# A decoder trunk layer on one core: half of the pairs' weight sums by accumulating transfers, the squares' sums pinned one part later, sigmoids behind the next pair's first copy

## The chip, the cores and the metric

The kernel runs on one core of a Trainium2 chip. The core has a matrix engine (PE, with its weight loads listed apart as PEld), a vector engine (DVE), a scalar engine (ACT), GpSimd (POOL) and a sync engine (SP); SP and POOL also issue transfers, POOL those that add onto what already lies in SBUF. The metric is the device time of one execution in microseconds (us), lower is better. The median of three runs is compared.

## The reference

One layer of a decoder over 512 tokens of 1024 channels. The parts that the change touches are the layer norm of the convolution branch, the two gates and their merge, and the up-projection of the channel mixer:

```python
u = _rmsnorm(h, norm1_g[l])
proj = u @ w_in[l]
a_glu, q, k, v, r, g_low, gate_a, gate_b = _split_cols(proj)
...
c = _causal_dwconv(c, conv_dw_w[l], conv_dw_b[l])
c = jax.nn.silu(_layernorm(c, conv_ln_g[l], conv_ln_b[l]))
y_conv = c @ w_conv_out[l]
...
y_gla = o @ w_gla_out[l]
merged = jax.nn.sigmoid(gate_a) * y_conv + jax.nn.sigmoid(gate_b) * y_gla
h = h + merged @ w_o[l]
u2 = _rmsnorm(h, norm2_g[l])
z = _causal_dwconv(u2 @ w_ffn_up[l], ffn_dw_w[l], ffn_dw_b[l])
h = h + (jax.nn.silu(z[..., :FFN_DIM]) * z[..., FFN_DIM:]) @ w_ffn_down[l]
```

## The kernel before

**Products.** Every fp32 operand is split into a rounded high part (`whi`, copied by ACT) and the remainder (`wlo`, subtracted by DVE); a product is three matmuls (`mm3`, lines 448 to 450). A weight tile `w[m]` is 128 x 1024: eight blocks of 128 input channels for one tile of 128 output channels. Its left half holds input blocks 0 to 3, its right half blocks 4 to 7. `split_weight` makes `whi` and `wlo` from the loaded tile `raw` (lines 355, 356 for sums and pairs, 385, 390 for plain tiles). Four `raw` buffers go round.

**Pairs.** Six pairs of gate tiles (`pair_7`, list `MERGE`) and eight pairs of up-projection tiles (`up_plan`) are computed by seven half products instead of eight (`two_tiles`, line 1164). Each needs four weights in the order x1, x3, x2, x4. With p and q the two tiles of a pair, x1 is p itself; x3 is the tile `three`, whose left half is p.left + q.left and whose right half is p.left + q.left + q.right; x2 is q with its left half replaced by q.left + q.right; x4 is the half tile p.left + q.left + q.right + p.right. `two_sums` (line 324) makes these sums with GpSimd adds of 128 x 512 (line 327): three of them when x1 has been split, one when x3 has been split. The fourth overwrites the left half of `three`, which x3 has read by then, and reads p.right, so p's buffer is held until then.

**Steps of a pair on PE.** x1: products a11 into bank x, a12 into bank z. x3: n2 onto x, s1 into y. x2: n3 onto x, s4 onto y. x4: a22 onto x. Between them `put` (line 1171, ACT) copies the partial sum of a bank out, and `combine` (line 1174, DVE) adds or subtracts; the next product onto the same bank waits for that. Half or whole products of other tiles stand between the parts of a pair (`BEHIND`: `w_gla`, later `w_conv`; in the up-projection plain `w_up` tiles).

**Merge stage and due times.** While the gates' pairs run, the layer norm of the convolution branch is worked off piece by piece. `norm_chain` is a list of (cost, work). Each call of `weight` gives room to `fill` (2.5 for a part of a pair, 5 for a tile), and pieces are popped while room is positive. `ln_center` (eight of them: a subtraction on DVE, line 860, a square on ACT, line 862, an addition on DVE, line 866) comes first; `ln_var` sums the squares over the channels by eight small matmuls (`token_sums`, line 837) and takes a root on GpSimd (line 500); `ln_rstd` spreads it (line 844); eight `ln_out` follow (lines 878 to 889, with a Silu on ACT, line 880). Before the change the last `ln_center` costs 5 and one empty piece of 2.5 stands before `ln_var`. By these numbers `ln_var` falls due at the x2 weight of the second pair, `ln_rstd` at the first `w_gla` tile of the third pair, and the last `ln_out` at x1 of the fourth pair. The instructions of one engine are put in order by a planner that works with its own cost model, unless a line pins them (`keep_in_program_order`, or `issue_after(i)`, which puts the instructions of a block behind `i` on `i`'s engine).

**Sigmoids.** When a gate pair is done, `pair_7` calls `sigmoid` for both tiles at once (line 1255, ACT).

**Up-projection.** When an up-projection pair is done, `value` runs the three-tap convolution of the first tile (`ffn_conv`: ACT line 1475, two DVE taps of line 1477) and a Silu (line 1482); `third_ahead` splits the x3 of the next pair early; `second_of_pair` runs the convolution of the second tile and what follows. `issue_after(third)` puts the DVE work of `second_of_pair` behind that x3's subtraction, where there was one.

Of the kernel before, what the change touches and what calls it, by code (L numbers as in the profile page):

```python
# [15 lines left out]
ALU = mybir.AluOpType  # L16

P = 128
D = 1024
T = 512  # L20
# [25 lines left out]
RATE = 5.0  # L46
# [29 lines left out]
def trunk_layer(ctx: ExitStack, tc: tile.TileContext, a: dict, out: bass.AP):  # L76
    nc = tc.nc
# [26 lines left out]
    def heap(dt=F32):  # L104
        return hp.tile([P, T], dt, tag="h", name=nm("h"))

    def tmp(n=T):
        return tp.tile([P, n], F32, tag="tmp", name=nm("tmp"), bufs=5)
# [10 lines left out]
    def mm_bank():  # L119
        return ps.tile([P, T], F32, tag="mm", name=nm("mm"), bufs=5)  # L120

    def ax_bank():
        return ps.tile([P, T], F32, tag="ax", name=nm("ax"), bufs=3)
# [10 lines left out]
    ones = cp.tile([P, P], F32, name="ones")  # L134
# [101 lines left out]
    ready, raws = [], []  # L236
    pair_raws = {}
# [29 lines left out]
    def raw_tile():  # L267
        return wp.tile([P, D], F32, tag="raw", name=nm("raw"), bufs=4)
# [50 lines left out]
    def two_operand(name, p, q, part):  # L319

        raws = pair_raws[name, p]
        return {"x1": lambda: raws[0], "x3": lambda: raws[2], "x2": lambda: raws[1], "x4": lambda: raws[2][:, :T]}[part]()

    def two_sums(name, p, q, part):

        def add(out, x, y):
            work = nc.gpsimd.tensor_tensor(out, x, y, ALU.add)  # L327
            if name == "w_up":
                tc.keep_in_program_order(work)

        left, right = slice(0, T), slice(T, D)
        if part == "x1":
            one, two = pair_raws[name, p]
            three = raw_tile()
            pair_raws[name, p].append(three)
            add(three[:, left], one[:, left], two[:, left])
            add(three[:, right], three[:, left], two[:, right])
            add(two[:, left], two[:, left], two[:, right])
        if part == "x3":
            one, _, three = pair_raws[name, p]  # L340
            add(three[:, left], three[:, right], one[:, right])

    def split_weight(halves=False, between=None):

# [54 lines left out]
    def third_ahead():  # L399

        n = used[0] + LOOK
        if n == len(ready) < len(order) and order[n][0] == "two" and order[n][1][-1] == "x3":
            split_weight()
            return two_low[0]
# [147 lines left out]
    start = tc.manual_schedule(engines=START)  # L552
# [175 lines left out]
    acc = mm_bank()  # L728
# [7 lines left out]
    acc = mm_bank()  # L736
# [74 lines left out]
    for k in range(KT):  # L811
# [4 lines left out]
        c = heap()  # L816
# [17 lines left out]
    def token_sums(s):  # L834
        b = ax_bank()
        for t in range(NT):
            nc.tensor.matmul(b[:, t : t + 1], s[:, t * P : (t + 1) * P], ones[:, 0:1], start=True, stop=True)
        return b[:, :NT]

    def spread(v):  # L840
# [18 lines left out]
    def ln_center(k):  # L859
        nc.vector.tensor_tensor(conv[k], stat["mean"], conv[k], ALU.add)  # L860
        sq = btmp()
        nc.scalar.activation(sq, conv[k], AF.Square)
        if k == 0:
            stat["sq"] = sq
        else:
            nc.vector.tensor_tensor(stat["sq"], stat["sq"], sq, ALU.add)  # L866
# [30 lines left out]
    def norm_chain():  # L897
        chain = [(RATE, ln_parts)]
        chain.append((0, ln_mean))
        chain.extend((2, lambda k=k: ln_center(k)) for k in range(KT))  # L900
        chain[-1] = (RATE, chain[-1][1])
        chain.append((2.5, lambda: None))
        chain.append((RATE, ln_var))
        chain.append((2.5, lambda: None))
        chain.append((0, ln_rstd))
        chain.extend((2.5, lambda k=k: ln_out(k)) for k in range(KT))
        return chain
# [17 lines left out]
    for k in range(KT):  # L925
        s = slice(k * P, (k + 1) * P)
# [323 lines left out]
    part = [None] * KT  # L1250
    gas = {}

    def sigmoid(m, acc):
        g = heap()
        nc.scalar.activation(g, acc, AF.Sigmoid)
        return g
# [13 lines left out]
    def tile_of(name, m, ks, acc=None):  # L1270
        if acc is None:
            acc = (weight(name, m), mm_bank())
        col_tile(acc[0], outs[name][0](), acc[1], ks=ks)
        if KT - 1 in ks:
            outs[name][1](m, acc[1])
        return acc
# [5 lines left out]
    half_of = [range(KT // 2), range(KT // 2, KT)]  # L1282
    open_tiles = {}

    def pair_7(n):
        (name, p, q), behind = MERGE[n], BEHIND[n]
        unit = two_tiles(name, p, q, lambda: merge_acts, mm_bank)
        if behind[0][0] == "w_conv":
            while chains:
                fill(1)  # L1290
        for j in range(4):
            while urgent and j and len(urgent) > (5 if j == 1 else 0):
                urgent.pop(0)[1]()
            done = next(unit)
            if j == 3:
                third_ahead()
                for m, c in zip((p, q), done):
                    (part if name == "w_gb" else gas)[m] = sigmoid(m, c)
            for proj, m, half in behind[j : j + 1]:
                open_tiles[proj, m] = tile_of(proj, m, half_of[half], open_tiles.get((proj, m)))  # L1300

# [170 lines left out]
    def ffn_conv(acc, m):  # L1472
        z = tmp()
        w = [pp[:, PP_FW + m * FW + j : PP_FW + m * FW + j + 1] for j in range(FW)]
        nc.scalar.activation(z, acc, AF.Identity, bias=pp[:, PP_FB + m : PP_FB + m + 1], scale=w[2])  # L1475
        for j, s in ((1, 1), (0, 2)):
            nc.vector.scalar_tensor_tensor(z[:, s:], acc[:, : T - s], w[j], z[:, s:], ALU.mult, ALU.add)  # L1477
        return z

    def value(i, acc):  # L1480
        za = ffn_conv(acc, i)
# [113 lines left out]

    gain3 = None
    banks, values, units = {}, {}, {}
    third = None
    for gi, pairs in enumerate(GROUPS):
        acts = []  # L1600
        if gi == 0:

            ws = [weight("w_up", j, 0) for i in pairs[0] for j in (i, FT + i)]
            accs = [mm_bank() for _ in ws]
            for j, lo in [(j, lo) for lo in (0, H) for j in range(3)]:
                late = {(1, 0): (KT - 1, 2), (2, 0): (MID, 3)}.get((j, lo))
                at = {late[0]: lambda t=late[1]: to_channels(normed[t], u2, t)} if late else {}
                col_tile(ws[j], acts2, accs[j], lo, lo + H, at)
            col_tile(ws[3], acts2, accs[3])
            p, q = pairs[0]  # L1610
            w = first_gated(p, value(p, accs[0]), accs[1])
            found = first_of_pair(w)
            up_acts, sums = ffn_sums()
            s1_n2, of_s1, s4, of_n2, of_s4, n3, of_n3 = sums
            sums = [s1_n2, of_n2 + of_s1, s4 + n3, of_n3 + of_s4]

            def some_sums():
                for _, work in sums.pop(0) if sums else ():
                    work()

            some_sums()
            acts.append(second_of_pair(q, value(q, accs[2]), accs[3], w, found))
            some_sums()
        else:
            found = first_of_pair(w)
        for what, i, *rest in up_plan(gi):
            if what == "tile":
                if 0 in rest[0]:
                    banks[i] = (weight("w_up", i), mm_bank())
                wt, acc = banks[i]  # L1630
                col_tile(wt, acts2, acc, ks=rest[0])
                if KT - 1 in rest[0] and i < FT:
                    values[i] = value(i, acc)
            if what == "part":
                if rest[0] == "x1":
                    units[i] = two_tiles("w_up", i, FT + i, lambda: up_acts, ax_bank)
                done = next(units[i])
                if done:
                    values[i] = value(i, done[0])
                    banks[FT + i] = (None, done[1])  # L1640
                    third = third_ahead()
            if what == "first":
                w = first_gated(i, values.pop(i), banks.pop(FT + i)[1])
                if any(i in pair for pair in pairs):
                    found = first_of_pair(w)
            if what == "second":
                with tc.issue_after(third.ins) if third else ExitStack():
                    acts.append(second_of_pair(i, values.pop(i), banks.pop(FT + i)[1], w, found))
                third = None
            if what in ("first", "second"):  # L1650
                some_sums()
        if gi < len(GROUPS) - 1:
            seven("w_down", pairs, acts, lambda t, n, c: None)
        else:
            gain3 = load_gain("final_g")
            seven("w_down", pairs, acts, last_complete, last_at, True)
# [90 lines left out]
```

## Time and profile before

| what | us |
|---|---|
| three runs | 831.57, 830.49, 829.85 |
| median | 830.49 |
| the profiled execution | 834.48 |
| its span, first to last instruction | 832.8 |
| outside the span in it | 1.7 |
| DVE busy | 717.5 |
| ACT busy | 450.1 |
| POOL busy | 149.4 |

The profile's page begins with the busy time of each engine. Its strip of 40 slices gives each engine's share of a slice (20.8 us) in tenths. Among the costliest groups are the plain product lines, and the GpSimd adds of the pairs:

```profile
L448 PE MATMUL mm<-uh,wlo 128*128 128x512 f32 (+1 forms) x672 | 244.5, 364 | 0.0
L327 POOL TENSOR_TENSOR raw<-raw,raw 128x512 f32<-128x512 f32 x42 | 68.2, 1623 | 222.6 <-DVE wlo L356 127.8
...
L1171 ACT COPY tmp<-mm 128x256 f32<-128x256 f32 x48 | 17.7, 368 | 34.0 <-PE mm L450 33.5
```

A row reads: line, engine, operation, what is written and read, shapes, count; then busy us, mean ns of one; then the idle time just before these instructions and what ended most of it. In views by time, a row is start, duration, engine, line, operation, and in brackets the idle time before it and its releaser. In tables by stage, each engine has its busy time and count, then the granted PE clock (1.00 is full), the busy share of the DMA engines and GB/s.

### The profile page before, as it was taken

What the parts mean: (1) busy time and instruction counts of PE and PEld (TensorE: products, weight loads), DVE (VectorE), ACT (ScalarE), POOL (GpSimd) and SP (SyncE); (2) the same over time, 40 slices, a digit from 0 to 9 for tenths busy, and PEclk for the clock granted to TensorE, in tenths of its full rate; (3) what the DMA queues carried; (4) which work ended last, traced back from release to release, by engine and by line L of the source; (5) the groups of instructions that cost most, each with busy time, mean ns of one, the idle gap of its engine ahead of it and who ended that gap; (6) DMA issues with size and microseconds to landing.
All of it is one profiled execution on the core that took longest, in us unless ns stands there. A gap on an engine that the chain in (4) does not pass through costs nothing.

```text
span 832.8 us, 11561 instructions
## 1 busy us (share of the span) xinstructions
PE 819.7 (98%) x4325; PEld 707.6 (85%) x4325; DVE 717.5 (86%) x1161; ACT 450.1 (54%) x666; POOL 149.4 (18%) x133
## 2 busy tenths in 40 slices
PE   8999999999999999899999999999999999999996
PEld 6888888888888889889988898899889988899885
DVE  5689999998989599685778889979984999789996
ACT  5744447656563446494444546556444664456654
POOL 1000010001100213335000200221133301513012
PEclk9999999999999999899999999999999999999999
DMA  7355672563433113223458633046743356324762
GB/s 289 112 123 149 151 185 98 128 152 101 105 100 109 43 50 103 92 87 102 160 144 228 177 102 102 26 136 172 145 130 102 130 146 141 129 84 157 189 128 102
DMA packets 30616, 106.27 MB, mean 128 GB/s; under 512 B 3464, under 2 KB 3600, under 8 KB 30560
## 3 DMA queue, kind: packets, MB, share of 16 engines
q1 hardware_dynamic: 24800, 85.35, 30.4%
q0 software_dynamic: 5760, 20.19, 14.5%
q8 instruction: 34, 0.56, 0.3%
q14 instruction: 22, 0.18, 0.1%
HBM read 103.42 MB, written 2.10 MB: 127 GB/s over the span
## 4 chain that ended last, share of the span: by engine, by line
PE 87%; DVE 8%; issue 2%; ACT 1%; DMA 1%; SPq 0%; POOL 0%; POOLq 0%; ACTq 0%; DVEq 0%
PE mm L448 25%; PE mm L449 25%; PE mm L450 25%; PE ax L450 2%; PE ax L448 2%; PE ax L449 2%; PE mm L662 2%; DVE wlo L356 1%; DMA pp<-in_pp_dram 1%; PE ax L1062 1%; DVE btmp L866 1%; DVE tmpq L1129 1%; DVE wlo L390 1%; PE ax L1064 1%; PE ax L1043 1%
## 5 line engine op out<-in xcount | busy, mean ns | idle before, releaser
L448 PE MATMUL mm<-uh,wlo 128*128 128x512 f32 (+1 forms) x672 | 244.5, 364 | 0.0
L449 PE MATMUL mm<-ul,whi 128*128 128x512 f32 (+1 forms) x672 | 242.3, 361 | 0.0
L450 PE MATMUL mm<-uh,whi 128*128 128x512 f32 (+1 forms) x672 | 241.9, 360 | 0.0
L450 PEld LDWEIGHTS mm<-uh,whi 128*128 128x128 f32 x672 | 126.7, 189 | 19.4
L448 PEld LDWEIGHTS mm<-uh,wlo 128*128 128x128 f32 x672 | 127.0, 189 | 19.1 <-DVE tmp L1174 0.2
L449 PEld LDWEIGHTS mm<-ul,whi 128*128 128x128 f32 x672 | 127.0, 189 | 18.7
L385 ACT CAST whi<-raw 128x1024 fp32r<-128x1024 f32 x86 | 89.6, 1046 | 61.6 <-PE mm L450 38.7
L356 DVE TENSOR_TENSOR wlo<-raw,whi 128x1024 fp32r<-128x1024 f32 x80 | 96.9, 1217 | 27.2 <-ACT whi L355 23.0
L327 POOL TENSOR_TENSOR raw<-raw,raw 128x512 f32<-128x512 f32 x42 | 68.2, 1623 | 222.6 <-DVE wlo L356 127.8
L390 DVE TENSOR_TENSOR wlo<-raw,whi 128x1024 fp32r<-128x1024 f32 x70 | 89.1, 1277 | 16.2 <-ACT whi L385 16.0
L355 ACT CAST whi<-raw 128x1024 fp32r<-128x1024 f32 x80 | 76.3, 958 | 37.6 <-PE mm L450 27.9
L783 DVE SCALAR_TENSOR_TENSOR c<-h,pp,c 128x255 f32<-128x255 f32 (+14 forms) x120 | 57.2, 477 | 3.6 <-ACT c L779 3.3
L783 DVE SCALAR_TENSOR_TENSOR c<-aside,btmp,c 128x255 f32<-128x255 f32 (+14 forms) x120 | 57.2, 477 | 2.8 <-ACT c L779 2.7
L783 DVE SCALAR_TENSOR_TENSOR aside<-h,pp,aside 128x255 f32<-128x255 f32 (+6 forms) x112 | 53.4, 477 | 0.0
L355 ACT CAST whi<-kept 128x1024 fp32r<-128x1024 f32 (+1 forms) x32 | 31.8, 996 | 31.1 <-DVE kept L310 14.8
L1477 DVE SCALAR_TENSOR_TENSOR tmp<-mm,pp,tmp 128x511 f32<-128x511 f32 (+1 forms) x56 | 41.5, 744 | 4.0 <-ACT tmp L1475 3.9
L356 DVE TENSOR_TENSOR wlo<-kept,whi 128x1024 fp32r<-128x1024 f32 (+1 forms) x32 | 37.9, 1186 | 4.3 <-ACT whi L355 4.3
L1171 ACT COPY tmp<-mm 128x256 f32<-128x256 f32 x48 | 17.7, 368 | 34.0 <-PE mm L450 33.5
L1394 DVE TENSOR_TENSOR hres<-hres,mm 128x512 f32<-128x512 f32 (+1 forms) x49 | 32.4, 672 | 3.3 <-PE mm L450 2.0
L1475 ACT ACTIVATE tmp<-mm,pp 128x512 f32<-128x512 f32 x28 | 21.7, 774 | 18.8 <-PE mm L450 18.6
L387 ACT ACTIVATE wlo<-raw 128x1024 fp32r<-128x1024 f32 x16 | 16.8, 1059 | 22.1 <-PE mm L448 22.1
L1477 DVE SCALAR_TENSOR_TENSOR tmp<-tmp,pp,tmp 128x511 f32<-128x511 f32 (+1 forms) x32 | 27.1, 905 | 0.1
(350 smaller groups left out, 1792.3 us busy)
## 6 DMA issues: line engine op xcount, KB each, us to landing
raw<-in_w_up_dram SPq DMA_DIRECT2D x44, 512.0 KB, 3.5
raw<-in_w_glu_dram SPq DMA_DIRECT2D x16, 512.0 KB, 4.8
raw<-in_w_down_dram SPq DMA_DIRECT2D x15, 512.0 KB, 3.9
kept<-in_w_down_dram POOLq DMA_DIRECT2D x10, 512.0 KB, 6.5
raw<-in_w_v_dram SPq DMA_DIRECT2D x8, 512.0 KB, 5.7
raw<-in_w_qk_dram SPq DMA_DIRECT2D x8, 512.0 KB, 3.4
raw<-in_w_r_dram SPq DMA_DIRECT2D x8, 512.0 KB, 4.5
wlo<-in_w_r_dram POOLq DMA_DIRECT2D x8, 512.0 KB, 8.0
```

Source lines behind the costliest of these rows:

```text
L327: work = nc.gpsimd.tensor_tensor(out, x, y, ALU.add)
L355: nc.scalar.copy(hi, raw)
L356: two_low[:] = [nc.vector.tensor_tensor(lo, raw, hi.bitcast(F32), ALU.subtract)]
L385: nc.scalar.copy(hi, raw)
L390: pace[0] = nc.vector.tensor_tensor(lo, raw, hi.bitcast(F32), ALU.subtract)
L448: nc.tensor.matmul(acc, ll, rh, start=first, stop=False, **kw)
L449: nc.tensor.matmul(acc, lh, rl, start=False, stop=False, **kw)
L450: nc.tensor.matmul(acc, lh, rh, start=False, stop=last, **kw)
L783: nc.vector.scalar_tensor_tensor(out[:, j:], x[:, : half_t - j], w, out[:, j:], ALU.mult, ALU.add)
L1394: done = nc.vector.tensor_tensor(hres[t, n][:, c], hres[t, n][:, c], acc[:, c], op)
L1475: nc.scalar.activation(z, acc, AF.Identity, bias=pp[:, PP_FB + m : PP_FB + m + 1], scale=w[2])
L1477: nc.vector.scalar_tensor_tensor(z[:, s:], acc[:, : T - s], w[j], z[:, s:], ALU.mult, ALU.add)
```

## The change

There are four edits. (1) Of the four sums of a pair, the third (q.left + q.right) and the fourth (x4) are no longer GpSimd adds but transfers that POOL issues, reading the right half of q or p once more from DRAM and adding it onto the tile in SBUF. x4 now stands in the right half of `three`, which already holds the other three terms, so the fourth sum no longer reads p's buffer. (2) The matmuls of `token_sums` are pinned in program order; the last `ln_center` costs 2 and four empty pieces of 2.5 follow, so that the room between it and `ln_var` is 12 instead of 7.5. (3) In the first three gate pairs the two sigmoids are traced after the next pair's first part (its `put` included) instead of at the pair's end; in the last three they stay at the pair's end, one call later. (4) In the up-projection the DVE work of `second_of_pair` is also put behind the last tap of the first tile's convolution.

```diff
     def two_operand(name, p, q, part):
-        return {..., "x4": lambda: raws[2][:, :T]}[part]()
+        return {..., "x4": lambda: raws[2][:, T:]}[part]()

     def two_sums(name, p, q, part):
...
             add(three[:, left], one[:, left], two[:, left])
             add(three[:, right], three[:, left], two[:, right])
-            add(two[:, left], two[:, left], two[:, right])
+            nc.gpsimd.dma_start(two[:, left], a[name][q][:, right], accum_op=ALU.add)
         if part == "x3":
-            one, _, three = pair_raws[name, p]
-            add(three[:, left], three[:, right], one[:, right])
+            nc.gpsimd.dma_start(pair_raws[name, p][2][:, right], a[name][p][:, right], accum_op=ALU.add)

     def token_sums(s):
...
-            nc.tensor.matmul(b[:, t : t + 1], s[:, t * P : (t + 1) * P], ones[:, 0:1], start=True, stop=True)
+            product = nc.tensor.matmul(b[:, t : t + 1], s[:, t * P : (t + 1) * P], ones[:, 0:1], start=True, stop=True)
+            tc.keep_in_program_order(product)

         chain.extend((2, lambda k=k: ln_center(k)) for k in range(KT))
-        chain[-1] = (RATE, chain[-1][1])
-        chain.append((2.5, lambda: None))
+        chain += [(2.5, lambda: None)] * 4
         chain.append((RATE, ln_var))

+    complete_pairs = []
     def pair_7(n):
...
             done = next(unit)
+            if j == 0 or n >= 3:
+                while complete_pairs:
+                    complete_pairs.pop(0)()
             if j == 3:
                 third_ahead()
-                for m, c in zip((p, q), done):
-                    (part if name == "w_gb" else gas)[m] = sigmoid(m, c)
+                def sigmoids(done=done):
+                    for m, c in zip((p, q), done):
+                        (part if name == "w_gb" else gas)[m] = sigmoid(m, c)
+                complete_pairs.append(sigmoids)
+                if n >= 3:
+                    complete_pairs.pop()()

     def ffn_conv(acc, m):
...
-            nc.vector.scalar_tensor_tensor(z[:, s:], acc[:, : T - s], w[j], z[:, s:], ALU.mult, ALU.add)
+            taps_at[:] = [
+                nc.vector.scalar_tensor_tensor(z[:, s:], acc[:, : T - s], w[j], z[:, s:], ALU.mult, ALU.add)
+            ]
...
                     values[i] = value(i, done[0])
                     banks[FT + i] = (None, done[1])
-                    third = third_ahead()
+                    third = [taps_at[0], third_ahead()]
...
             if what == "second":
-                with tc.issue_after(third.ins) if third else ExitStack():
+                with ExitStack() as order_of:
+                    for ins in third:
+                        if ins:
+                            order_of.enter_context(tc.issue_after(ins.ins))
                     acts.append(second_of_pair(i, values.pop(i), banks.pop(FT + i)[1], w, found))
-                third = None
+                third = []
```

More of the change, by code (lines that the diff above doesn't have):

```diff
@@ L321, in two_operand @@
         raws = pair_raws[name, p]
-        return {"x1": lambda: raws[0], "x3": lambda: raws[2], "x2": lambda: raws[1], "x4": lambda: raws[2][:, :T]}[part]()
+        return {"x1": lambda: raws[0], "x3": lambda: raws[2], "x2": lambda: raws[1], "x4": lambda: raws[2][:, T:]}[part]()
     def two_sums(name, p, q, part):
@@ L1476, in ffn_conv @@
         for j, s in ((1, 1), (0, 2)):
-            nc.vector.scalar_tensor_tensor(z[:, s:], acc[:, : T - s], w[j], z[:, s:], ALU.mult, ALU.add)
+            taps_at[:] = [
+                nc.vector.scalar_tensor_tensor(z[:, s:], acc[:, : T - s], w[j], z[:, s:], ALU.mult, ALU.add)
+            ]
         return z
+    taps_at = []
     def value(i, acc):
@@ L1646, in trunk_layer @@
             if what == "second":
-                with tc.issue_after(third.ins) if third else ExitStack():
+                with ExitStack() as order_of:
+                    for ins in third:
+                        if ins:
+                            order_of.enter_context(tc.issue_after(ins.ins))
                     acts.append(second_of_pair(i, values.pop(i), banks.pop(FT + i)[1], w, found))
-                third = None
+                third = []
             if what in ("first", "second"):
```

## The prediction

> **What bounds the kernel now.** I read the page first, for the engine that sets the time.
>
> ```profile
> PE 819.7 (98%) x4325; PEld 707.6 (85%) x4325; DVE 717.5 (86%) x1161; ACT 450.1 (54%) x666; POOL 149.4 (18%) x133
> ...
> PEclk9999999999999999899999999999999999999999
> ```
>
> PE is busy 819.7 of 832.8 us. The change leaves its products as they are, so it can only win PE's idle time and time at a lower clock; the clock strip has one dip, in the seventeenth slice (333 to 354 us). Second view: the whole list of waits of the matmul engine inside the run, of which these two rows lie where the change works.
>
> ```profile
> PE ax L837 <- DVE btmp L866: 2.1, 1, 2.1
> ...
> PE mm L448 <- ACT tmp L1171: 1.1, 2, 0.6
> ```
>
> PE waits 2.1 us once for the squares' sum, and twice, 1.1 us together, for an evacuation by ACT. Third view: the stages around the dip (busy times, then clock, DMA share, GB/s).
>
> ```profile
> 334.00:337.00 3.00, 0.90 (x9) 0.73 (x7) 2.59 (x2) 0.00 (x0) 2.92 (x2) 1.00 0.24 94
> 337.00:344.00 7.00, 7.00 (x30) 6.61 (x30) 1.62 (x4) 1.04 (x1) 2.91 (x3) 0.51 0.01 2
> 344.00:348.00 4.00, 4.00 (x28) 3.67 (x28) 2.27 (x3) 1.72 (x3) 0.00 (x0) 1.00 0.39 131
> ```
>
> The clock is 0.51 for the 7 us that follow the wait and full again after them: 7 x (1 - 0.51) = 3.4 us of PE work lost. The page shows no such dip beside the two waits of at most 0.6 us. So the wait for the squares costs 2.1 + 3.4 = 5.5 us, and the two evacuations 1.1. **6.6 us is about all there is to win.**
>
> **Edit 2, the squares' sums.** The rows around the wait, in order of time:
>
> ```profile
> 333.92 3.80 POOL L327 TENSOR_TENSOR raw<-raw,raw 128x512 f32<-128x512 f32 x2 [6.89 <-ACT btmp L862]
> ...
> 334.12 0.28 PE L448 MATMUL mm<-sumsq,wlo 128*128 128x256 f32 x1
> ...
> 334.24 0.28 PE L449 MATMUL mm<-xq,whi 128*128 128x256 f32 x1
> ...
> 334.84 1.75 DVE L866 TENSOR_TENSOR btmp<-btmp,btmp 128x512 f32<-128x512 f32 x1
> ...
> 336.73 1.50 PE L837 MATMUL ax<-ones,btmp 128*128 128x1 f32 x8 [2.10 <-DVE btmp L866]
> ...
> 338.09 0.56 PE L448 MATMUL mm<-sumsq,wlo 128*128 128x256 f32 x1
> ...
> 338.90 1.01 POOL L500 TENSOR_TENSOR rstd<-mean,mhalf 128x4 f32<-128x4 f32 x1
> ...
> 345.70 0.28 PE L448 MATMUL mm<-uh,wlo 128*128 128x256 f32 x1
> ```
>
> DVE ends the last addition at 334.84 + 1.75 = 336.59; PE, which had reached the small matmuls inside x2's first product, starts them at 336.73. By the costs of the chain, `ln_var` moves from the x2 weight to the x4 weight of the second pair, whose first matmul is the one at 345.70. Taking out the wait (2.1), the slow clock (3.4) and the small matmuls (338.09 - 336.73 = 1.4), PE would be there at 345.7 - 6.9 = 338.8. That is 2.2 us after 336.59, so the wait goes. It would come back only if the chain of centers ran over 2.2 us later than now. It rather runs earlier:
>
> ```profile
> L866 DVE TENSOR_TENSOR btmp<-btmp,btmp x7: 677/681/1774, 319.6 to 334.8; 128x512 f32<-128x512 f32 x7
> ```
>
> This addition takes 681 ns at the median and 1774 beside the GpSimd adds. What is late next: the root, the spreading matmuls and eight `ln_out`. The spreading stays due at the third pair's first `w_gla` tile, behind x4 (12 matmuls) and x1 (24), which at the 0.12 us from start to start of the rows at 334.12 and 334.24 is 4.3 us after the sums: enough for a root of 1.01 us. The `ln_out` move one part later, the last to x3 of the fourth pair; its first reader is a `w_conv` tile of the fifth. I take -5.5 us; bounds -5.5 and 0.
>
> **Edit 3, the sigmoids.** ACT at the third pair's end:
>
> ```profile
> 368.59 0.37 ACT L1171 COPY tmp<-mm 128x256 f32<-128x256 f32 x1
> ...
> 369.92 1.28 ACT L1255 ACT_TABLE_LOAD   x1
> 371.21 1.15 ACT L1255 ACTIVATE h<-tmp 128x512 f32<-128x512 f32 x2
> 372.27 0.35 ACT L1171 COPY tmp<-mm 128x256 f32<-128x256 f32 x1
> ```
>
> A table load of 1.28 and two sigmoids of 1.15 together stand before the copy at 372.27, which PE awaits for half of the 1.1 us. The edit puts that copy first: -0.55. Against it: with the later `ln_out`, the Silu of the seventh stands before these sigmoids and that of the eighth behind them, so the function changes back and forth, up to two more loads, 2.6 us of ACT.
>
> ```profile
> 360.00:380.00 20.00, 19.44 (x138) 17.91 (x137) 16.35 (x21) 16.03 (x23) 7.92 (x5) 1.00 0.25 81
> ```
>
> ACT has 4.0 us free in that stage, and the loads fit on average; if this cover fails, they delay evacuations by up to 2.6 us. Bounds 0 and +2.6; I take +0.4, nearer to the covered end.
>
> **Edit 4, the taps.** The second evacuation wait:
>
> ```profile
> 662.09 2.09 DVE L356 TENSOR_TENSOR wlo<-raw,whi 128x1024 fp32r<-128x1024 f32 x1
> ...
> 664.10 3.76 DVE L1477 SCALAR_TENSOR_TENSOR tmp<-tmp,pp,tmp 128x511 f32<-128x511 f32 x4
> ...
> 667.29 0.63 ACT L1482 ACTIVATE tmp<-tmp 128x512 f32<-128x512 f32 x1 [2.72 <-DVE tmp L1477]
> ...
> 667.78 1.21 DVE L356 TENSOR_TENSOR wlo<-raw,whi 128x1024 fp32r<-128x1024 f32 x1
> ...
> 667.83 0.76 ACT L1475 ACTIVATE tmp<-mm,pp 128x512 f32<-128x512 f32 x1
> 668.49 0.36 ACT L1171 COPY tmp<-mm 128x256 f32<-128x256 f32 x1
> ...
> 668.90 0.39 PE L448 MATMUL mm<-xq,wlo 128*128 128x256 f32 x1 [0.53 <-ACT tmp L1171]
> ```
>
> The four taps belong to two convolutions in turn. In sequence the first pair of taps ends half of 3.76, 1.9 us, earlier, and with it the Silu and the copy behind: more than the 0.53 that PE waits. -0.53; bounds -0.53 and 0. The second tile's taps come later, but their results wait for the next down-projection.
>
> **Edit 1, the sums.** It removes 14 in-place adds and 14 others:
>
> ```profile
> L327 POOL TENSOR_TENSOR raw<-raw,raw x42: 1279/1450/3411, 283.6 to 756.7; 128x512 f32<-128x512 f32 x42
> ...
> L327 POOL TENSOR_TENSOR raw<-raw x14: 1271/2044/2277, 286.2 to 753.3; 128x512 f32<-128x512 f32 x14
> ```
>
> By the medians that is 14 x 2.04 + 14 x 1.45 = 49 us of POOL, none of it on PE's path, and with it part of DVE's slowing. It adds 28 transfers of 256 KB. Their nearest rows:
>
> ```profile
> kept<-in_w_down_dram POOLq DMA_DIRECT2D x2, 256.0 KB, 7.4
> ...
> raw<-in_w_down_dram POOLq DMA_DIRECT2D x1, 256.0 KB, 3.9
> ...
> L300 POOL DMA_DIRECT2D raw<-in_w_down_dram x6: 844/862/1132, 588.9 to 801.5; - x6
> ```
>
> Each holds POOL for 0.86 us, less than the add, and lands 3.9 to 7.4 us after its issue instead of 1.5 to 2.0. Who waits: x2's copy by ACT, and x4's. POOL's second add, x2's copy and x2's first product in the two tightest up-projection pairs:
>
> ```profile
> 657.33 3.53 POOL L327 TENSOR_TENSOR raw<-raw,raw 128x512 f32<-128x512 f32 x2 [11.86 <-DVE wlo L356]
> ...
> 663.52 1.05 ACT L355 CAST whi<-raw 128x1024 fp32r<-128x1024 f32 x1
> ...
> 673.95 0.28 PE L448 MATMUL mm<-btmpq,wlo 128*128 128x256 f32 x1
> ...
> 749.76 3.53 POOL L327 TENSOR_TENSOR raw<-raw,raw 128x512 f32<-128x512 f32 x2 [11.86 <-DVE wlo L356]
> ...
> 755.95 1.05 ACT L355 CAST whi<-raw 128x1024 fp32r<-128x1024 f32 x1
> ```
>
> The transfer can go at 657.33 + 3.53 = 660.86; x2 is needed by PE 13.1 us later, and copy (1.05) and subtraction (1.21) leave 10.8: x2 itself is in time. But its copy stood 2.7 us after that point (same in the other pair), so in the old ACT order it would wait for the landing, and the Silu, the convolution's start and the evacuation at 668.49 stand behind it. Working back from 668.37 (668.90 less the wait of 0.53) through 0.36 + 0.76 + 0.63 + 1.05 = 2.8 us of ACT, the landing has to be at 665.6, 4.7 us after issue. At 3.9 nothing is lost; at 7.4 PE waits 2.7 us. That holds for ACT's old order; the planner prices transfers, and for those that it already has, ACT waits little:
>
> ```profile
> ACT whi L355 <- DMA kept<-in_w_down_dram: 3.7, 2, 2.8
> ```
>
> Two waits in all, off the matmuls' list. So the copy is likely put behind the evacuation; I take +0.5, between 0 and 2 x 2.7 = +5.4. x4's transfer waits for x3's subtraction, as the add did. One gain is left at nothing: p's buffer comes free about a part earlier, and the pairs' loads wait less.
>
> ```profile
> SPq L253 <- POOL raw L327: 62.5, 10, 12.5
> ```
>
> No product's wait in PE's list is for a pair's load, so this only adds cover.
>
> By the Trainium skill's "DMA: Bandwidth & Descriptors" (Anatomy of one DMA), a transfer from GpSimd costs about 2.0 us plus its bytes over 436 GB/s, an estimate of 2.6 us for 256 KB; then no copy would wait and this term would be 0 instead of 0.5. The rows above, 3.9 to 7.4, disagree, and I keep them.
>
> **Sum.** -5.5 - 0.55 + 0.4 - 0.53 + 0.5 = -5.7 us, made against the profiled 834.48 (span 832.8 and 1.7 around it), hence 828.8 for a profiled execution. The profiled one is 4.0 above the median of the runs; taken from the median 830.49 the forecast is **824.8**.
>
> **Rivals.** *ACT becomes the short bound* (17%): the table loads stall PE for their whole 2.6, and one pair's transfer for another 0.6 beyond my 0.5: 824.8 + 2.2 + 0.6 = 827.6. For it: ACT's 16.03 of 20 us; against: 4 us free.
>
> *The clock does not come back* (6%): the wait goes, but the dip has another cause, such as the small matmuls themselves, which keep PE nearly idle wherever they stand. Then 3.4 of the gain is missing: 828.2. For it: the clock row begins with these matmuls, after only 2.1 us of idling; against: the strip dips nowhere else, though other matmuls as small follow soon after (line 844). The Trainium skill's "TensorE: Matmul & The Clock Gate" (Part 1) puts the drop after an idle window of about 3.4 us; by that rule alone a wait of 2.1 would not have halved the clock, which speaks for this rival, while the trace's row shows the halving right behind the wait.
>
> *The change doesn't do what it says* (5%): pinned small matmuls still meet an unfinished sum and PE waits as before: only edits 3 and 4 count, 824.8 + 5.5 = 830.3, no change.
>
> *Slower* (13%): the landings of the third sum hold ACT in the two tight pairs. At 7.4 us PE waits 2.7 in each, longer than the 2.1 that halved the clock, so 3.4 more each: 2 x 6.1 = 12.2 in place of my 0.5, 836.5. It decides when landings pass 4.7 us with the copy still ahead of the evacuation, and costs more than the whole gain once both waits are long enough for the clock.
>
> **Numbers.** The forecast has 59%. A difference under 0.2% (1.7 us) can't be told from none. Faster: 59 + 17 + 6 = 82%; same 5%; slower 13%. The range, 822.5 to 829.0, holds the first three cases: at the low end the two positive terms are nothing and the runs win some of DVE's relief (830.5 - 6.6 - 1.4), at the high end the 828.2 of the third case with some more waits.
>
> **What would show it.** Right: no wait of line 837 on line 866, clock 1.00 through 333 to 350; no wait of a product on line 1171 near 366 and 660; half the adds of line 327; ACT waits of line 355 on `raw` transfers short, with no PE wait behind. Wrong: a new PE wait on line 1171 or 355 beside a POOL transfer of `raw`, a second dip of the clock, or three table loads between 345 and 380 with PE waiting.

## The result and the profile after

| kernel | median us | runs | range us | ratio to before (95%) |
|---|---|---|---|---|
| before | 830.89 | 17 | 829.50 to 832.53, and one of 1372.05 | 1 |
| changed | 834.26 | 17 | 830.61 to 838.03 | 1.0041 (1.0028 to 1.0054) |

The change makes the kernel slower by 0.4%, 3.4 us, where 5.7 us of gain were forecast. Single executions far above all others (1372.05 here, and below one each of `e1_only`, `e2_only` and the kernel before) are left out of the ratios. The profiled execution of the changed kernel took 830.61 us, which is the fastest of its 17; that of the kernel before had taken 834.48, above all of the usual runs beside it. The two profiles therefore show a gain of 3.9 us where the medians show a loss of 3.4. What follows reads the profile for places and the medians for sizes.

The page of the changed kernel: busy time of each engine, the clock strip, and the group of the pairs' adds.

```profile
PE 816.2 (98%) x4325; PEld 704.7 (85%) x4325; DVE 701.2 (85%) x1161; ACT 450.6 (54%) x666; POOL 120.6 (15%) x133
...
PEclk9999999999999999999999999999999999999999
...
L328 POOL TENSOR_TENSOR raw<-raw,raw 128x512 f32<-128x512 f32 x28 | 41.8, 1493 | 139.3 <-DVE wlo L356 55.3
```

The adds have gone from 56 to 28, POOL is 29 us less busy (the adds took 95.0 us and now take 41.8; 28 issues at 0.86 us are new) and DVE 16 us; the dip of the clock is gone. Lines are a little further down than before: the add is line 328, the transfers are lines 339 (x2) and 341 (x4), the convolution is lines 1487 and 1490 and its Silu line 1498; lines 355 (copy of a weight) and 1171 (evacuation) have kept their numbers. The stage in which PE had waited for the squares' sum, by windows (busy times of PE, PEld, DVE, ACT and POOL, then clock, DMA share, GB/s):

```profile
334.00:337.00 3.00, 3.00 (x27) 2.96 (x26) 2.16 (x3) 0.00 (x0) 2.92 (x3) 1.00 0.21 49
337.00:344.00 7.00, 7.00 (x51) 6.51 (x50) 4.13 (x6) 3.85 (x5) 2.72 (x3) 1.00 0.62 169
```

PE is busy throughout and the clock is full: edit 2 does here what was forecast. In PE's list of waits the row for line 837 has gone, and the evacuations are first:

```profile
PE mm L448 <- ACT tmp L1171: 2.1, 2, 1.6
...
PE mm L448 <- DVE tmp L1174: 0.3, 1, 0.3
```

They cost 2.1 us in two waits, 1.1 before. One is near 561 us, the other near 665, each in the last pair of a group of the up-projection. These two are called the closing pairs below: no plain tile stands between their x3, x2 and x4, so that x4 is prepared, and its copy put in line on ACT, as soon as the products of x3 are called. ACT in the second of them, in order of time:

```profile
658.67 1.05 ACT L355 CAST whi<-raw 128x1024 fp32r<-128x1024 f32 x1
660.33 0.63 ACT L1498 ACTIVATE tmp<-tmp 128x512 f32<-128x512 f32 x1 [0.60 <-DVE tmp L1490]
660.86 0.76 ACT L1487 ACTIVATE tmp<-mm,pp 128x512 f32<-128x512 f32 x1
664.19 0.62 ACT L355 CAST whi<-raw 128x512 fp32r<-128x512 f32 x1 [2.57 <-DMA raw<-in_w_up_dram]
664.72 0.37 ACT L1171 COPY tmp<-mm 128x256 f32<-128x256 f32 x1
```

The copy of x2 (658.67) meets no wait. The half-size copy at 664.19 is that of x4: it waits 2.57 us for the new transfer (issued at 658.92, landed 5.2 us later), and the evacuation that PE awaits stands behind it: PE waits 1.56 us. In the kernel before, these two stood the other way round: the evacuation at 668.49, and then, in its view by time,

```profile
668.74 0.63 ACT L355 CAST whi<-raw 128x512 fp32r<-128x512 f32 x1
```

The landings of x4's transfer over the whole run (view of line 341 of the changed kernel) are within what was forecast:

```profile
DMA to landing us min/median/max: 3.8/4.1/5.2
```

The 5.2 is not beyond the 3.9 to 7.4 expected; what differs is who stands behind the reader.

### The profile page after: what moved, and what is told of

Same layout as the page of the kernel before. It is cut to its first block, busy times and chain, and to the rows that moved or that the text cites. A ratio compares the mean times of both kernels' runs of the same rounds, so it can differ in the third digit from the quotient of the medians.

```text
span 828.9 us, 11601 instructions
## 1 busy us (share of the span) xinstructions
PE 816.2 (98%) x4325; PEld 704.7 (85%) x4325; DVE 701.2 (85%) x1161; ACT 450.6 (54%) x666; POOL 120.6 (15%) x133
## 4 chain that ended last, share of the span: by engine, by line
PE 94%; DVE 2%; DMA 1%; ACT 1%; SPq 0%; issue 0%; POOL 0%; POOLq 0%; ACTq 0%
PE mm L448 27%; PE mm L449 27%; PE mm L450 27%; PE ax L450 2%; PE ax L449 2%; PE ax L448 2%; PE mm L662 2%; DMA pp<-in_pp_dram 1%; PE ax L1062 1%; DVE tmp L1490 1%; PE ax L1043 1%; PE ax L1064 1%; DVE wlo L356 1%; PE ax L1030 0%; PE ax L1029 0%; PE ax L529 0%
## 5 line engine op out<-in xcount | busy, mean ns | idle before, releaser
L356 DVE TENSOR_TENSOR wlo<-raw,whi 128x1024 fp32r<-128x1024 f32 x80 | 91.2, 1145 | 37.2 <-ACT whi L355 32.7
L390 DVE TENSOR_TENSOR wlo<-raw,whi 128x1024 fp32r<-128x1024 f32 x70 | 86.7, 1243 | 16.3 <-ACT whi L385 16.3
L328 POOL TENSOR_TENSOR raw<-raw,raw 128x512 f32<-128x512 f32 x28 | 41.8, 1493 | 139.3 <-DVE wlo L356 55.3
L449 PE MATMUL mm<-wlo,sh 128*128 128x512 f32 x66 | 25.8, 390 | 0.0
```

Source lines behind the costliest of these rows:

```text
L356: two_low[:] = [nc.vector.tensor_tensor(lo, raw, hi.bitcast(F32), ALU.subtract)]
L390: pace[0] = nc.vector.tensor_tensor(lo, raw, hi.bitcast(F32), ALU.subtract)
L449: nc.tensor.matmul(acc, lh, rl, start=False, stop=False, **kw)
```

## The experiments

Fourteen runs of twelve kernels (`again`, `look_a` and `look_b` are the changed kernel once more). Runs named together were timed on the same chip against the same runs of the kernel before, whose median was 830.91 beside the first four, 831.37 beside the next four and 831.34 beside the four after them; ratios carry a 95% interval.

### Edit 1 alone, the rest alone, and each transfer alone

```diff
 e1_only: the kernel before, with
+            nc.gpsimd.dma_start(two[:, left], a[name][q][:, right], accum_op=ALU.add)
+            nc.gpsimd.dma_start(pair_raws[name, p][2][:, right], a[name][p][:, right], accum_op=ALU.add)
 e234: the changed kernel, with all four sums as adds
+            add(two[:, left], two[:, left], two[:, right])
+            add(three[:, left], three[:, right], one[:, right])
 x2_transfer: the changed kernel, with the x4 sum as an add
+            add(three[:, left], three[:, right], one[:, right])
 x4_transfer: the changed kernel, with the x2 sum as an add
+            add(two[:, left], two[:, left], two[:, right])
```

> Before plus edit 1 alone (two of the four sums of a pair by transfers). Theory T (transfers): ACT's copies of x2 and x4 wait in ACT's order for landings, evacuations stand behind them, and the stalls often pass the length that halves the PE clock; then this alone is slower than before by about what the whole change lost or more, 834 to 837 us, with PE waits on line 1171 beside transfers of raw. Rival O (order): the loss of the whole change comes from edits 2 to 4 (tables, pinned sums, taps); then this one stays within 1 us of before, 830 to 832.

> The changed kernel with all four sums by GpSimd adds again (edits 2, 3 and 4 alone). Theory T: no landing in ACT's way, so at or under before, 828.5 to 830.5, and the runs lie closer together than those of the changed kernel. Rival O: as slow as the whole change, 833 to 835.

> The changed kernel with the fourth sum (x4) by GpSimd again, in the left half as before; only the third sum (x2) by transfer. If x4's transfers are what costs (theory T4: their copy stands right before an evacuation in the pair near 660 us), 829 to 831; if x2's are (T2, the prediction's slower rival), 833 to 835; if both cost in like parts, about 832.

> The changed kernel with the third sum (x2) by GpSimd again; only the fourth sum (x4) by transfer. T4: 833 to 835, with the wait of an evacuation behind x4's copy near 660 us in the trace. T2: 829 to 831. Both: about 832.

| kernel | median us | ratio to before (95%) |
|---|---|---|
| e1_only | 830.25 | 0.9987 (0.9974 to 0.9999) |
| e234 | 829.85 | 0.9989 (0.9981 to 0.9998) |
| x2_transfer | 829.98 | 0.9986 (0.9976 to 0.9996) |
| x4_transfer | 829.62 | 0.9985 (0.9976 to 0.9993) |

All four are about a microsecond faster than before, and none shows the loss. So neither edit 1 nor edits 2 to 4 nor one of the transfers is slow by itself. Every theory was contradicted by one of its runs: theory T by e1_only, rival O by e234, T2 by x2_transfer and T4 by x4_transfer. The loss needs both transfers together with one of the other edits.

e1_only has the old order on ACT, and shows the stall that the slower rival had named, at its place. Its ACT by time:

```profile
662.04 1.05 ACT L354 CAST whi<-raw 128x1024 fp32r<-128x1024 f32 x1 [4.16 <-issue]
...
664.18 0.36 ACT L1170 COPY tmp<-mm 128x256 f32<-128x256 f32 x1
664.44 0.62 ACT L354 CAST whi<-raw 128x512 fp32r<-128x512 f32 x1
```

Here the copy of x2 holds ACT for 4.16 us, ahead of the evacuation at 664.18, and PE waits 1.8 us in this one pair, with the clock at half for 3.4 us behind it; x4's copy is behind and harmless. e234 has the new order, with x4's sum as an add:

```profile
662.79 0.61 ACT L356 CAST whi<-raw 128x512 fp32r<-128x512 f32 x1
664.04 0.37 ACT L1172 COPY tmp<-mm 128x256 f32<-128x256 f32 x1 [0.65 <-DVE tmp L1491]
```

x4's copy is ahead of the evacuation here too, without waiting, because the add has ended. Its PE list has the row

```profile
PE mm L449 <- ACT tmp L1172: 1.1, 4, 0.3
```

four waits of at most 0.3 us; the evacuation is released there by a convolution tap on DVE, not by x4's copy. The order that is harmless with an add is the one that waits with a transfer.

x4_transfer has that order too, with x4's sum as a transfer, and it shows the same stall, only shorter:

```profile
662.36 0.62 ACT L355 CAST whi<-raw 128x512 fp32r<-128x512 f32 x1 [2.13 <-DMA raw<-in_w_up_dram]
662.89 0.37 ACT L1171 COPY tmp<-mm 128x256 f32<-128x256 f32 x1
```

PE waits 1.1 us here, and for no evacuation in the first closing pair, where x4's transfer lands after 3.8 us. What differs is the landing: 4.8 us at most, against 5.2 and, in the three other traces of the changed kernel, 6.1 to 6.9. The three loads that SP issues just ahead of it land in 4.5 to 5.1 us, and in 6.0 to 9.0 where x2's sum is a transfer as well. By this one trace, the second kind of transfer is needed because with it the landing is later; how it makes it later is not shown.

### The changed kernel again, and with one edit undone

```diff
 again: the changed kernel, nothing else
 no_e2: edit 2 undone
-        chain += [(2.5, lambda: None)] * 4
+        chain[-1] = (RATE, chain[-1][1])
+        chain.append((2.5, lambda: None))
 (and the small matmuls of token_sums not pinned)
 no_e3: the sigmoids at each pair's end
-            if j == 0 or n >= 3:
+            if j == 0 or n >= 0:
-                if n >= 3:
+                if n >= 0:
 no_e4: the second convolution not put behind the first one's last tap
-                    third = [taps_at[0], third_ahead()]
+                    third = [third_ahead()]
```

> The changed kernel itself once more, on the chip of the other runs of this call. Theory I (interaction): both kinds of transfers together with one of the edits 2 to 4 make an order that the parts don't have; then it is slow again, 833 to 836 us, and a trace of a usual execution shows one or more stretches at half clock that the first trace (its fastest execution) lacked. Rival C (chance): the earlier 834 was of that chip or hour; then 829.5 to 830.5, like the parts.

> The changed kernel with edit 2 undone (the squares' sums unpinned and due a part earlier). If edit 2 is the partner of the transfers (its later layer-norm pieces crowd ACT and DVE in the gate pairs): 829.5 to 830.5. If edit 3 or 4 is: 833 to 836.

> The changed kernel with edit 3 undone (sigmoids at the pair's end again). If edit 3 is the partner of the transfers: 829.5 to 830.5. If edit 2 or 4 is: 833 to 836.

> The changed kernel with edit 4 undone (the second tile's work behind x3's subtraction alone). If edit 4 is the partner of the transfers (it is what acts in the up-projection pairs, where the changed trace's longest PE wait lies, 1.6 us near 665): 829.5 to 830.5. If edit 2 or 3 is: 833 to 836.

| kernel | median us | ratio to before (95%) |
|---|---|---|
| again | 834.11 | 1.0044 (1.0027 to 1.0060) |
| no_e2 | 838.47 | 1.0081 (1.0063 to 1.0098) |
| no_e3 | 834.17 | 1.0032 (1.0013 to 1.0051) |
| no_e4 | 829.99 | 0.9988 (0.9976 to 1.0000) |

The loss repeats. Undoing edit 3 changes nothing. Undoing edit 2 costs another 4.4 us (838.47 against 834.11), which neither of its two expected outcomes had; so edit 2 is a gain inside a slower kernel. Undoing edit 4, which had been costed at a gain of 0.53 and nothing at worst, takes 4.1 us of loss away. PE's waits in no_e2, where the old wait is back beside the new ones:

```profile
PE mm L448 <- ACT tmp L1171: 4.3, 2, 2.6
...
PE ax L837 <- DVE btmp L866: 2.2, 1, 2.2
```

ACT of no_e4 in the second closing pair:

```profile
663.27 1.05 ACT L355 CAST whi<-raw 128x1024 fp32r<-128x1024 f32 x1 [4.13 <-issue]
...
665.41 0.36 ACT L1171 COPY tmp<-mm 128x256 f32<-128x256 f32 x1
665.67 0.63 ACT L355 CAST whi<-raw 128x512 fp32r<-128x512 f32 x1
```

This is the order of e1_only: without edit 4, x4's copy (665.67) stands behind the evacuation, and the wait falls on x2's copy instead. So edit 4, by ending the first convolution's taps and its Silu earlier, changes which weight copy the planner puts ahead of the evacuation. This trace is of no_e4's slowest execution (832.95), in which PE waits 1.8 us for this evacuation and runs at half clock for 3.4 us behind it. By its median the wait on x2 usually costs less than the wait on x4, but perhaps not nothing: the kernel with all four edits and neither wait (x4_behind, below) is 2.1 us faster than no_e4.

### Each edit alone, and the order on ACT mended

```diff
 e2_only: the kernel before with edit 2; e4_only: the kernel before with edit 4
 closing_pool: the changed kernel; in the two closing pairs the x4 sum is an add
+CLOSING = {("w_up", 7), ("w_up", 21)}
+            if (name, p) in CLOSING:
+                add(three[:, left], three[:, right], one[:, right])
+            else:
                 nc.gpsimd.dma_start(pair_raws[name, p][2][:, right], a[name][p][:, right], accum_op=ALU.add)
 x4_behind: the changed kernel; in the two closing pairs x4's copy is put behind the evacuations
-        prefetch(ahead)
+        prefetch(1 if name == "two" and j[0] == "w_up" and j[-1] == "x3" and order[used[0] + 1][0] == "two" else ahead)
...
-            nc.scalar.copy(c, acc[:, :H])
+            copied[:] = [nc.scalar.copy(c, acc[:, :H])]
...
-        put(c2[:, t1], x)
+        put(c2[:, t1], x); first = copied[0]
...
-        w = weight("two", (name, p, q, "x2"))
+        with tc.issue_after(first.ins) if name == "w_up" and len(ready) == used[0] + 1 else ExitStack(): w = weight("two", (name, p, q, "x2"))
```

> Before plus edit 2 alone (the squares' sums pinned and due a part later). The prediction gave it 5.5 us. Undoing it in the changed kernel cost 4.4. If that gain holds in usual executions: 825 to 827. If the before kernel in its usual executions mostly lacks the long wait (its profiled execution, 834.5, was slower than all but one of its timed runs) and only the changed one needs the edit: 829.5 to 830.5.

> Before plus edit 4 alone (the second tile's DVE work behind the first tile's taps). Theory H: without a transfer for x4 there is nothing to wait for at the head of ACT's queue; it takes at most 0.5 us off, 830 to 831. If edit 4 is bad by itself: 832 to 835.

> The changed kernel with x4's sum by GpSimd add in those two pairs alone (2 of 28 transfers taken back, into the left half as before). Theory H: 828.5 to 830.5, like x4_behind. Rival B: 833 to 834, since 26 of 28 transfers remain.

> The changed kernel with one thing moved: in the two pairs that close a group of the up-projection, ACT's copy of x4 stands behind the two evacuations of the part x3 instead of ahead of the first; all transfers stay. Theory H (head of ACT's queue): the copy that waits for x4's landing, at two places of the kernel, is the whole loss; then 828.5 to 830.5, no PE wait on line 1171 near 561 and 665, and x4's landing there as late as before (5 to 6 us) without effect. Rival B (traffic): 28 more transfers slow loads and landings in many places; then 832 to 834.

| kernel | median us | ratio to before (95%) |
|---|---|---|
| e2_only | 828.89 | 0.9974 (0.9962 to 0.9987) |
| e4_only | 833.02 | 1.0016 (1.0000 to 1.0032) |
| closing_pool | 829.21 | 0.9972 (0.9960 to 0.9983) |
| x4_behind | 827.85 | 0.9956 (0.9939 to 0.9972) |

In x4_behind the first line delays preparing x4 until x2 is called, and the others pin its copy behind the first evacuation of x3. Rival B, the traffic of 28 more transfers, is refuted by both mends; x4_behind even came out below the expected range. The other two runs missed theirs: e2_only lies between its two ranges, and e4_only, without any transfer in the pairs, is slower than the 830 to 831 of theory H, in the range for "bad by itself". Its list of PE's waits has

```profile
PE mm L448 <- ACT tmp L1171: 1.7, 5, 0.6
```

four of them 0.27 us long, in the up-projection's pairs, as in e234, where the kernel before had one of 0.53. So edit 4's gain does not come, landings or not. The remainder of its 1.7 us (833.02 against 831.34) is not explained.

Two different mends of the same two places, one that takes the landing away and one that takes the queue away, both end the loss. With x4_behind all four edits and all 28 transfers stay, and the kernel is 6.3 us faster than the changed one on the same chip (834.11 - 827.85) and faster than the kernel before. Its ACT in the second closing pair, and the landing row of its x4 transfers:

```profile
659.19 0.63 ACT L1498 ACTIVATE tmp<-tmp 128x512 f32<-128x512 f32 x1 [0.32 <-DVE tmp L1490]
659.73 0.76 ACT L1487 ACTIVATE tmp<-mm,pp 128x512 f32<-128x512 f32 x1
661.66 0.37 ACT L1171 COPY tmp<-mm 128x256 f32<-128x256 f32 x1 [1.17 <-DVE tmp L1490]
...
664.24 0.37 ACT L1171 COPY tmp<-mm 128x256 f32<-128x256 f32 x1 [0.78 <-PE mm L450]
664.73 0.62 ACT L355 CAST whi<-raw 128x512 fp32r<-128x512 f32 x1
```

```profile
DMA to landing us min/median/max: 3.7/4.2/6.7
```

The transfer is not faster here: its longest landing, 6.7 us, is above the 5.2 of the changed kernel's profile. What has moved is the copy, and x4's subtraction with it, from ahead of the evacuation to behind the second one. PE's windows there:

```profile
660.00:664.00 4.00, 4.00 (x28) 3.63 (x27) 4.00 (x7) 1.48 (x3) 0.00 (x0) 1.00 0.92 239
664.00:668.00 4.00, 4.00 (x28) 3.63 (x27) 4.00 (x9) 3.21 (x6) 0.00 (x0) 1.00 0.21 50
```

PE is busy in all of both windows. So the loss is not the transfer's time by itself but what stands behind its first reader on ACT.

### What a usual execution of the changed kernel looks like

Its profile was of its fastest execution, so the unchanged kernel was profiled twice more.

> The changed kernel, one more profiled execution, to see a usual one (both traces of it so far were its fastest executions, 830.6 and 832.1). Theory H: its time above 828.2 is made up of the PE waits at the two closing pairs (near 561 and 665) and of half-clock windows of 3.4 us (1.7 us each) behind them; for 834, two waits over 2 us and one or two windows. If it is above 833 with smaller waits there, the loss has a further place.

> As look_a: a second draw. The sum of the waits near 561 and 665 and of 1.7 us for each half-clock window behind them, added to 828.2, gives its time within 1 us, if theory H holds.

look_a took 832.66 us, look_b 837.04; the kernel before beside them 830.19. look_b's ACT in the second closing pair:

```profile
664.09 0.76 ACT L1487 ACTIVATE tmp<-mm,pp 128x512 f32<-128x512 f32 x1
669.08 0.62 ACT L355 CAST whi<-raw 128x512 fp32r<-128x512 f32 x1 [4.22 <-DMA raw<-in_w_up_dram]
669.60 0.36 ACT L1171 COPY tmp<-mm 128x256 f32<-128x256 f32 x1
```

and its PE, by time and by windows:

```profile
666.42 0.39 PE L450 MATMUL mm<-uh,whi 128*128 128x512 f32 x1
670.02 0.51 PE L448 MATMUL mm<-xq,wlo 128*128 128x256 f32 x1 [3.21 <-ACT tmp L1171]
670.32 0.41 PE L449 MATMUL mm<-usq,whi 128*128 128x256 f32 x1
...
673.65 0.28 PE L450 MATMUL ax<-xq,whi 128*128 128x256 f32 x1
673.77 0.28 PE L448 MATMUL ax<-xq,wlo 128*128 128x256 f32 x1
```

```profile
668.00:672.00 4.00, 1.98 (x9) 1.98 (x10) 1.48 (x4) 1.41 (x3) 0.00 (x0) 0.77 0.04 12
672.00:676.00 4.00, 4.00 (x24) 3.74 (x23) 2.71 (x5) 2.42 (x5) 0.00 (x0) 0.81 0.36 104
```

PE waits 3.21 us, and then the same matmuls start 0.21 us apart instead of 0.12 until 673.5: the clock is halved for 3.4 us, which loses 1.7 us ((1 - 0.77) x 4 + (1 - 0.81) x 4). In look_b both closing pairs do this:

```profile
PE mm L448 <- ACT tmp L1171: 5.7, 2, 3.2
```

5.7 us of waits and 2 x 1.7 of slow clock are 9.1 us. Less that, look_b is at 827.9. In look_a the same waits are 3.3 us with one slow stretch of 1.7, and 832.66 less 5.0 is 827.7; in `again` 3.0 us with one, and 832.11 less 4.7 is 827.4; in the changed kernel's own profile 2.1 us with none, and 830.61 less 2.1 is 828.5. All four come within a microsecond of the 827.85 that x4_behind measures. The waits at two places and their slow clock thus make up the loss in four traces, from 830.61 to 837.04; the slowest execution, 838.03, was not profiled.

PE's wait at a closing pair follows from the landing of x4's transfer there: it is the landing less about 3.7 us. 4.2 us gave 0.56 and 5.2 gave 1.56 in the changed kernel's profile, 4.8 gave 1.12 in x4_transfer, 6.1 gave 2.48 in `again`, 6.3 gave 2.62 in look_a, 6.1 and 6.9 gave 2.44 and 3.21 in look_b. x4_behind, with 5.6 and 6.7, has no such wait.

The transfer in look_b's second closing pair was issued at 662.14. SP's issues shortly ahead of it:

```profile
657.71 0.33 SPq L257 DMA_DIRECT2D raw<-in_w_up_dram  x1
658.09 0.95 SPq L296 DMA_DIRECT2D kept<-in_w_down_dram  x2
659.14 0.37 SPq L296 DMA_DIRECT2D raw<-in_w_down_dram  x1
```

Its longest x4 landing is this one:

```profile
DMA to landing us min/median/max: 3.7/4.2/6.9
```

Those loads had 6.9 to 9.0 us to their landing in the same trace, so the transfer comes in behind a burst. That the burst makes it late fits. So does x2's transfer: it lands in 3.8 us in the changed kernel, where it is issued at 653.19, ahead of the first of the `w_down` loads (654.86), and in 7.8 in e1_only and no_e4, where it is issued 0.6 us behind it. But no run here moved the loads alone, so it stays an argument.

## Why the prediction was wrong

**The step that failed.** "So the copy is likely put behind the evacuation; I take +0.5", and the sentence after it, "x4's transfer waits for x3's subtraction, as the add did". The first was about x2's copy, which did stay ahead of the evacuation (658.67) and waited for nothing only because its transfer had landed, issued at 653.19 with 3.8 us to the landing. The second passed x4 over, and that is the wait that the sum lacks: it was put at nothing, and by `again` and x4_behind it costs 6.3 us. In the old order, x4's copy was indeed behind the evacuation (668.74). But the order was taken from the trace of before while another edit of the same change altered it: edit 4 brings the Silu forward, and in e4_only, e234, x2_transfer and the changed kernel alike the planner then has x4's copy ahead. With an add the copy is done before DVE releases the evacuation, and PE waits at most 0.3 us a place in e234; with a transfer PE waits for what the landing has beyond 3.7 us. That both edits are needed is shown by medians: no_e4 and e234, each with one of the two missing, are at 829.99 and 829.85, the kernel with both at 834.26. The interval for edit 1, 0 to +5.4, covered only a fixed order on ACT, and edit 4's bounds, -0.53 to 0, had no loss in them. Alone, edit 4 already leans to the slower side, 1.0016 (1.0000 to 1.0032): ending the first taps earlier did not let PE wait less, it made four small waits out of one.

**The slower rival, at 13%, had the mechanism and not the operand.** ACT's queue is held by a copy that waits for a landing, with an evacuation behind it, and the clock is halved after the longer waits: so it was priced, at 2.7 + 3.4 us a place. The operand was x4 instead of x2, the pairs were those near 561 and 665 instead of 660 and 753, and in the traces of the changed kernel a place costs 0.6 to 3.2 us of waiting and 0 or 1.7 of slow clock, not 3.4. Its own case, x2's copy in the pair near 660, does exist, in e1_only and no_e4 (4.16 and 4.13 us of ACT, 1.8 of PE and half clock behind it); e1_only's median shows no loss against before all the same, and no_e4's may hold part of it. Its point of decision, a landing past 4.7 us, was for x2; x4 loses from 3.7 on, and even the usual landing of 4.1 is past that.

**Edit 2 was right in mechanism and too large.** Wait and dip are gone, as forecast, and nothing late next shows up. But -5.5 was the price in one execution. By medians the edit alone gains 2.5 (e2_only: 828.89 against 831.34). The wait is not always there without it: e1_only's trace has none on line 837, and e4_only's has one of 1.1 us with the clock at 1.00 behind it. The mean granted clock of before's runs varies from 0.993 to 0.999, and the profiled one, at 0.993, is among the lowest: by that, most of them lack a dip of 7 us. Beside the new waits the edit is worth 4.4.

**The sum was carried over to a number it was not made for.** The prediction noted that the profiled execution is 4.0 us above the median, and still took the whole 5.7 from the median. By its low clock, part of those 4.0 us is the very dip that the change removes, and so that part was taken off twice. The same terms taken from 834.48 give 828.8; x4_behind, where the landings hold nothing up, has 827.85.

**Edit 3 was about neutral, as forecast, and its loads did not come.** With it undone the time is 834.17 against 834.11, and PE has no wait near 366 in that trace either. The prediction gave two more table loads as possible. The profile of after has one load for the Silus and one for the sigmoids, as before, with the two evacuations now ahead of the latter:

```profile
346.19 1.28 ACT L881 ACT_TABLE_LOAD   x1
...
362.97 0.37 ACT L1171 COPY tmp<-mm 128x256 f32<-128x256 f32 x1
...
364.18 0.38 ACT L1171 COPY tmp<-mm 128x256 f32<-128x256 f32 x1
364.58 1.28 ACT L1255 ACT_TABLE_LOAD   x1
```

**The other rivals.** "ACT becomes the short bound" fell with the missing loads. "The clock does not come back" fell too: the small matmuls now run between others at clock 1.00. "The change doesn't do what it says" fell with the same row. The landing as such was forecast well: 3.9 to 7.4 from three rows, 3.6 to 7.8 in the traces read here, with medians of 3.7 to 4.2, so the 2.6 us of the Trainium skill's "DMA: Bandwidth & Descriptors" (Anatomy of one DMA), from which no wait would have followed, was too short here.

## What to carry to other kernels

When an add on an engine becomes a transfer, don't ask only whether the data are in time for the matmul: look up what stands behind their first reader in its engine's queue, and ask whether another edit of the same change alters that order. A wait that is hidden by order, not by time, should have that order written down; here one ordering constraint at two places was worth 6.3 us. Before a sum goes from a profile to a median, look where that one execution lies among the runs, and take off what it has by chance.

## What was not expected of the hardware

- The granted clock was halved for 3.4 us, once for 7 (before), beside waits of PE of 1.8 us (e1_only, no_e4), 2.1 (before), 2.2 and 2.6 (no_e2), 2.5 (again), 2.6 (look_a) and 2.4 and 3.2 (look_b), but not beside one of 2.4 (no_e3), 1.7 (no_e2) or 1.6 (after). So a wait between 1.8 and 2.4 us may or may not cost 1.7 us more, which adds to the 7 us over which the same kernel spreads. The Trainium skill's "TensorE: Matmul & The Clock Gate" (Part 1) puts the drop after an idle window of about 3.4 us; in these rows less is enough.
- A transfer of 256 KB that adds onto SBUF mostly lands after 4.1 us, but the same one in the same place took 5.2 (after) and 6.9 us (look_b) to land from one execution to the next, with no change in the program.
- One profile of each kernel gave the wrong sign of the change: 834.48 before and 830.61 after, against medians of 830.89 and 834.26.
